# A small weight loaded as 16 lines of 1 KB in place of 128 lines of 128 B, and ScalarE's pause moved one group ahead, in a LoRA projection on one core

## Chip, cores, metric

The kernel runs on one core of a Trainium2 chip. The time is the device time of one execution in microseconds (us). All runs in this document count as undisturbed ("fast"): each is within 1.5% of the fastest of its kernel. Differences of 0.1 to 0.3 us are the subject, so eleven kernels were timed in five rounds and seven in three, always beside the kernel before on the same chip. Kernels of different rounds ran on different chips; each is compared with the kernel before of its own rounds. A profile shows one execution, and times in us from the start of its span.

A few words used below. A *packet* is one piece that one of the core's 16 DMA engines moves; the trace records start, duration, size and queue of each. A *load* goes from HBM to the core's SBUF memory, a *store* the other way. `x` is cut into four *chunks* of 8 MB, a chunk into 16 *groups* of 4 rows per partition.

## The reference

```python
x: (16, 2048, 256)   W: (256, 256)   lora_A: (256, 16)   lora_B: (16, 256)   lora_E: (16,)   # float32
y = x_flat @ W + scale * ((x_flat @ lora_A) * lora_E) @ lora_B                                # scale = 1
```

33.6 MB of `x` come in and 33.6 MB of `y` go out.

## The kernel before

The kernel folds the low-rank part into one weight, `weff = W + (A * E) @ B`, and then multiplies every group of `x` by it. For this it needs A transposed: `a_sb` holds A, TensorE turns it, VectorE scales it. SyncE issues all large transfers in the order of a list, and each chunk has a home in SBUF that the result overwrites. There are three homes for four chunks.

```python
ORDER = [
    ("A",),
    ("L", 0, 0, 16), ("L", 0, 16, 40), ("L", 0, 40, 64),      # loads: chunk, first row, last row
    ("L", 1, 0, 32), ("L", 1, 32, 64),
    ("L", 2, 0, 64),
    ("S", 0, 0, 40), ("S", 0, 40, 64),                        # stores
    ("L", 3, 0, 32), ("L", 3, 32, 64),                        # wait for the stores of chunk 0
    ("S", 1, 0, 64), ("S", 2, 2, 62), ("S", 3, 0, 64),
]
...
a_sb = sbuf("a_sb", [P, KT, R], FP32)                         # 128 partitions x 2 rows x 16
...
def drain(engine, n):                                         # waits for chunk 2's load, then n drains
    for op, landed in loaded.items():
        if op[1:3] == HELD:                                   # HELD = (2, 0)
            engine.wait_ge(landed, 16)
    for _ in range(n):
        engine.drain()
...
for g in range(N_GROUPS):                                     # ScalarE
    c, b = g // GPC, g % GPC * CG
    if (c, b) == HELD:
        drain(scalar, SCALAR_DRAINS)                          # 22
    scalar.wait_ge(s_y, g + 1)
    scalar.copy(out=home(c)[:, b:b + CG, :], in_=psum_y[g % NY][:])...
...
for t in range(KT):                                           # TensorE turns A: 2 x 128 columns
    ins = tensor.transpose(psum_y[0][:R, t, :P], a_sb[:, t, :], ident[:])
```

GpSimd holds chunk 2 back until the first store has landed. GpSimd and VectorE run some drains, empty instructions (8 to 34 ns in the median), while they stand there, and ScalarE runs its own when it comes to chunk 2. They are there for what the trace shows behind them: three packets of 8 KB in the queue that the page calls "instruction" (q14), at 67.83, 67.84 and 84.82 us, each 3 to 5 us after an engine's drains. I call them fetches. ScalarE's drains halt once, for 0.35 us between the 21st and the 22nd, and I take this pause for the sign of its fetch; the drains are meant to bring both into a time in which the engine idles.

Of the kernel before, what the change touches and what calls it, by code (L numbers as in the profile page):

```python
# [7 lines left out]
P = 128  # L8
FP32 = mybir.dt.float32
# [4 lines left out]
ROWS = 64  # L14
# [24 lines left out]
HELD = (2, 0)  # L39
# [3 lines left out]

VECTOR_DRAINS = 12
GPSIMD_DRAINS = 10
SCALAR_DRAINS = 22

CG = 4
GPC = ROWS // CG
# [8 lines left out]
def kernel(  # L58
# [13 lines left out]
    N, K = x_flat.shape  # L72
    M = out_flat.shape[1]
    R = lora_B.shape[0]
    KT = K // P
# [5 lines left out]
    sbuf, psum, sem = nc.alloc_sbuf_tensor, nc.alloc_psum_tensor, tc.alloc_semaphore  # L81
# [3 lines left out]
    ident = sbuf("ident", [P, P], FP32)  # L85

    w_sb = sbuf("w_sb", [P, KT, M], FP32)
    a_sb = sbuf("a_sb", [P, KT, R], FP32)
    b_sb = sbuf("b_sb", [R, M], FP32)
    e_sb = sbuf("e_sb", [R, 1], FP32)  # L90
    ate = sbuf("ate", [R, KT, P], FP32)
# [2 lines left out]
    psum_y = [psum(f"psum_y{i}", [P, CG, M], FP32) for i in range(NY)]  # L94
# [24 lines left out]
    def home(c):  # L119
        return homes[c % N_HOMES]  # L120

    sync, gpsimd, scalar, vector, tensor = nc.sync, nc.gpsimd, nc.scalar, nc.vector, nc.tensor
# [20 lines left out]
    def sync_program():  # L143
        for n, op in enumerate(ORDER):
            if op[0] == "A":
                a = lora_A.rearrange("(q t) r -> q t r", t=KT)
                ins = sync.dma_start(out=a_sb[:], in_=a).then_inc(set_up_loaded["a"], 16)  # L147
                opening.append(ins.ins.name)
                continue
            kind, c, s, e = op  # L150
            at_home = home(c)[:, s:e, :]
            if kind == "L":
                for st in stored:
                    if st[1] == c - N_HOMES and st[2] < e and s < st[3]:
                        sync.wait_ge(stored[st], 16)
                ins = sync.dma_start(out=at_home, in_=x_chunks[c, :, s:e, :]).then_inc(loaded[op], 16)
                if n == 1:
                    opening.append(ins.ins.name)
            else:
                sync.wait_ge(s_done, ends.index((c * ROWS + e - 1) // CG) + 1)  # L160
                sync.dma_start(out=y_chunks[c, :, s:e, :], in_=at_home).then_inc(stored.get(op, stored_rest), 16)
        sync.wait_ge(shared_stored, 16 * len(SHARES))
# [7 lines left out]
    def drain(engine, n):  # L170
        for op, landed in loaded.items():
            if op[1:3] == HELD:
# [3 lines that stand above are left out]
# [32 lines left out]
    def scalar_program():  # L208
        for name, to, of in (
            ("w", w_sb, W.rearrange("(q t) m -> q t m", t=KT)),  # L210
            ("b", b_sb, lora_B),
            ("e", e_sb, lora_E[:, None]),
        ):
            ins = scalar.dma_start(out=to[:], in_=of).then_inc(set_up_loaded[name], 16)
            opening.append(ins.ins.name)
        for g in range(N_GROUPS):
            c, b = g // GPC, g % GPC * CG
            if (c, b) == HELD:
                drain(scalar, SCALAR_DRAINS)
            scalar.wait_ge(s_y, g + 1)  # L220
            scalar.copy(out=home(c)[:, b:b + CG, :], in_=psum_y[g % NY][:]).then_inc(s_free[(g + NY) % UNROLL], 1)  # L221
            if (c, b + CG) == (SHARED, ROWS):
                scalar.drain().then_inc(s_shared, 1)
            if g in ends:
                scalar.drain().then_inc(s_done, 1)  # L225
# [23 lines left out]
    def tensor_program():  # L249
        def turn(i, result=None):  # L250
            words = stage[i % NS][:].bitcast(FP32)
            staged = s_stage[i % UNROLL]
            for b in range(CG):
                if b == 0:
                    tensor.wait_ge(staged, 1)
                if b == CG - 1 and result is not None:
                    tensor.wait_ge(s_free[result % UNROLL], 1)
                ins = tensor.transpose(psum_xt[i % NT][:, b, :], words[:, b, :], ident[:])  # L258
                if b == 0:
                    ins.then_inc(staged, -1)  # L260
            ins.then_inc(s_turned, 1)

        def multiply(i):
            turned, free = s_xt[i % UNROLL], s_free[i % UNROLL]
            for b in range(CG):
                for t in range(KT):
                    if b == t == 0:
                        tensor.wait_ge(turned, 1)
                    ins = tensor.matmul(  # L269
                        psum_y[i % NY][:, b, :],  # L270
                        xt[i % NX][:, b, t::KT],
                        weff[:, t, :],
                        start=(t == 0),
                        stop=(t == KT - 1),
                    )
                    if b == 0:
                        ins.then_inc((turned, free)[t], -1)
            ins.then_inc(s_y, 1)

        tensor.wait_ge(s_ident, 2)  # L280
        for i in range(WARM_UP):
            tensor.matmul(psum_y[1][:, :2, :], ident[:], ident[:, None, :].to_broadcast([P, 4, P]), start=True, stop=True)  # L282
        tensor.wait_ge(set_up_loaded["a"], 16)
        for t in range(KT):
            ins = tensor.transpose(psum_y[0][:R, t, :P], a_sb[:, t, :], ident[:])  # L285
        ins.then_inc(s_pe_set_up, 1)
        turn(0)
        tensor.wait_ge(set_up_loaded["b"], 16)
        tensor.wait_ge(s_ate, 1)
        for t in range(KT):  # L290
            ins = tensor.matmul(psum_y[1][:, t, :], ate[:, t, :], b_sb[:], start=True, stop=True)  # L291
        ins.then_inc(s_pe_set_up, 1)
        assert N_GROUPS % UNROLL == 0 and all(UNROLL % n == 0 for n in (NS, NX, NT, NY))
        with tensor.Fori(0, N_GROUPS // UNROLL):
            for i in range(UNROLL):
                turn(i + 1, i)
                multiply(i)
# [6 lines left out]
    with tc.tile_critical(no_gpsimd_drain=True):  # L304
        sync_program()
        gpsimd_program()
        scalar_program()
        vector_program()
        tensor_program()
# [35 lines left out]
```

## Time and profile before

| | before |
|---|---|
| median time (3 runs ahead of the prediction) | 161.29 us |
| bytes moved | 67.43 MB |
| floor (an estimate) at 27.1 GB/s per DMA engine, from 65,536 B in 2.418 us | 155.5 us |
| TensorE busy | 60% |
| share of SyncE's queue in the time of the 16 DMA engines | 97.4% |

The DMA engines move data from 1.0 us on without a visible gap (no slice of the page's DMA row is under 6), and TensorE stands idle for over a third of the time while they do (56 to 76 us, and from 122 us on). The page's chain of waits nevertheless names TensorE first:

```profile
PE 38%; DMA 33%; ACT 3%; POOL 1%; issue 1%; ACTq 0%; SPq 0%
```

A chain follows instructions and their semaphores. It can't see that a store, once issued, stands behind other stores in the queue.

### The profile page before, as it was taken

To read this page: it belongs to the slowest core of one execution; us is meant where nothing else is said; L and a number is where in the kernel's file an instruction comes from. 1 tells how busy PE (TensorE), PEld (TensorE's weight loads), DVE (VectorE), ACT (ScalarE), POOL (GpSimd) and SP (SyncE) were. 2 spreads that over 40 slices of the span, in tenths; PEclk is the share of its full clock that TensorE was granted. 3 is DMA by queue.
4 is the path that set the end of the run, shared out by engine and by line. 5 is a ranking of instruction groups with operands and counts; after the bars stand their busy time and mean duration, and the time that the engine had idled before them with its cause. 6 is when DMAs were issued, how large, how long until landed. Compare 5 with 4: busy or idle time off the path is not lost.

```text
span 160.0 us, 2070 instructions
## 1 busy us (share of the span) xinstructions
PE 96.5 (60%) x782; PEld 84.4 (53%) x782; DVE 45.4 (28%) x66; ACT 66.0 (41%) x65; POOL 69.3 (43%) x73
## 2 busy tenths in 40 slices
PE   2769999999999900000999999999994000000000
PEld 1246899999999900000789999999993000000000
DVE  0113355555555500000155555555550000000000
ACT  3001477777777720000257777777775000000000
POOL 1072577777787400002577777778762000000000
PEclk9999999999999995555599999999999555555555
DMA  7999999999969997999999999989979997989986
GB/s 269 427 448 436 412 440 467 451 393 418 631 262 524 475 311 328 403 420 434 412 465 428 401 475 426 532 377 410 524 308 446 480 485 305 544 342 481 441 360 262
DMA packets 2451, 67.43 MB, mean 421 GB/s; under 512 B 512, under 2 KB 528, under 8 KB 784
## 3 DMA queue, kind: packets, MB, share of 16 engines
q1 hardware_dynamic: 2016, 66.60, 97.4%
q0 software_dynamic: 224, 0.52, 0.9%
q10 hardware_dynamic: 208, 0.28, 0.6%
q14 instruction: 3, 0.02, 0.0%
HBM read 33.85 MB, written 33.55 MB: 421 GB/s over the span
## 4 chain that ended last, share of the span: by engine, by line
PE 38%; DMA 33%; ACT 3%; POOL 1%; issue 1%; ACTq 0%; SPq 0%
DMA out_dram<-home 28%; PE psum_y L269 24%; PE psum_xt L258 13%; DMA home<-in_x_dram 5%; ACT home L221 3%; POOL stage L200 1%; PE psum_y L291 1%; SPq L147 0%; ACTq L175 0%; ACTq L225 0%
## 5 line engine op out<-in xcount | busy, mean ns | idle before, releaser
L200 POOL CAST stage<-home 128x1024 bf16<-128x1024 f32 x64 | 66.6, 1042 | 48.6 <-PE psum_xt L258 22.1
L221 ACT COPY home<-psum_y 128x1024 f32<-128x1024 f32 x64 | 64.7, 1012 | 54.8 <-PE psum_y L269 54.8
L269 PE MATMUL psum_y<-weff,xt 128*128 128x256 bf16 x512 | 69.1, 280 | 0.0
L242 DVE COPY xt<-psum_xt 128x1024 bf16<-128x1024 bf16 x64 | 44.3, 692 | 66.2 <-PE psum_xt L258 66.2
L258 PE MATMUL psum_xt<-ident,stage 128*128 128x128 f32 x260 | 42.2, 286 | 22.3 <-POOL stage L200 22.3
L269 PEld LDWEIGHTS psum_y<-weff,xt 128*128 128x128 bf16 x512 | 51.5, 101 | 6.2
L258 PEld LDWEIGHTS psum_xt<-ident,stage 128*128 128x128 f32 x260 | 32.4, 148 | 25.2 <-issue 23.6
L282 PE MATMUL psum_y<-ident 128*128 128x512 f32 x4 | 3.8, 1101 | 2.9 <-POOL ident L180 2.9
L282 PEld LDWEIGHTS psum_y<-ident 128*128 128x128 f32 x4 | 1.2, 325 | 3.9 <-POOL ident L180 2.9
L230 DVE TENSOR_SCALAR ate<-psum_y,e_sb 16x256 f32<-16x256 f32 x1 | 0.5, 471 | 7.2 <-DMA e_sb<-in_lora_E_dram 7.2
L168 POOL DMA_DIRECT2D out_dram<-home x3 | 2.0, 676 | 1.0 <-PE psum_xt L258 1.0
L221 ACT ACT_TABLE_LOAD x1 | 1.3, 1283 | 2.1 <-SPq L304 2.1
L291 PE MATMUL psum_y<-b_sb,ate 16*128 16x256 f32 x4 | 2.1, 670 | 0.0
L291 PEld LDWEIGHTS psum_y<-b_sb,ate 16*128 16x128 f32 x4 | 1.2, 320 | 0.5 <-issue 0.3
L246 DVE TENSOR_TENSOR weff<-w_sb,psum_y 128x512 bf16<-128x512 f32 x1 | 0.7, 689 | 1.4 <-PE psum_y L291 1.4
L285 PEld LDWEIGHTS psum_y<-ident,a_sb 128*16 128x16 f32 x2 | 0.3, 138 | 1.2 <-issue 1.2
L178 POOL MEMSET ident<- 128x128 f32 x1 | 0.2, 205 | 1.7 <-SPq L304 1.7
L285 PE MATMUL psum_y<-ident,a_sb 128*16 128x128 f32 x2 | 0.6, 421 | 0.0
L180 POOL TENSOR_SCALAR_AFFINE_SELECT ident<-ident 128x128 f32<-128x128 f32 x1 | 0.3, 284 | 0.2 <-POOL ident L178 0.2
L326 POOL MEMSET const-float32-0.0<- 128x1 f32 x1 | 0.1, 94 | 0.2 <-issue 0.2
L326 POOL MEMSET const-bfloat16-1.0<- 128x1 bf16 x1 | 0.1, 97 | 0.0
L326 POOL MEMSET const-uint8-127<- 128x1 uint8 x1 | 0.1, 97 | 0.0
(1 smaller groups left out, 0.1 us busy)
## 6 DMA issues: line engine op xcount, KB each, us to landing
home<-in_x_dram SPq DMA_DIRECT2D x4, 4096.0 KB, 24.4
out_dram<-home SPq DMA_DIRECT2D x1, 7680.0 KB, 38.0
home<-in_x_dram SPq DMA_DIRECT2D x2, 3072.0 KB, 16.8
out_dram<-home SPq DMA_DIRECT2D x1, 5120.0 KB, 45.2
out_dram<-home SPq DMA_DIRECT2D x1, 3072.0 KB, 44.6
home<-in_x_dram SPq DMA_DIRECT2D x1, 2048.0 KB, 7.7
out_dram<-home POOLq DMA_DIRECT2D x1, 432.0 KB, 30.2
w_sb<-in_W_dram ACTq DMA_DIRECT2D x1, 256.0 KB, 2.8
```

The source lines that it names most:

```text
L168: engine.dma_start(out=ends_of(y_chunks[SHARED]), in_=ends_of(home(SHARED))).then_inc(landed, 16)
L200: gpsimd.tensor_copy(out=stage[g % NS][:], in_=home(c)[:, b:b + CG, :]).then_inc(s_stage[g % UNROLL], 1)
L221: scalar.copy(out=home(c)[:, b:b + CG, :], in_=psum_y[g % NY][:]).then_inc(s_free[(g + NY) % UNROLL], 1)
L230: vector.tensor_scalar(out=ate[:], in0=psum_y[0][:R, :KT, :P], scalar1=e_sb[:], scalar2=float(scale), op0=ALU.mult, op1=ALU.mult,).then_in ...
L242: vector.tensor_copy(out=xt[g % NX][:], in_=psum_xt[g % NT][:].bitcast(BF16)).then_inc(s_xt[g % UNROLL], 1)
L246: vector.tensor_add(out=weff[:], in0=w_sb[:], in1=psum_y[1][:, :KT, :]).then_inc(s_free[0], 1)
L258: ins = tensor.transpose(psum_xt[i % NT][:, b, :], words[:, b, :], ident[:])
L269: ins = tensor.matmul(psum_y[i % NY][:, b, :], xt[i % NX][:, b, t::KT], weff[:, t, :], start=(t == 0), stop=(t == KT - 1),)
L282: tensor.matmul(psum_y[1][:, :2, :], ident[:], ident[:, None, :].to_broadcast([P, 4, P]), start=True, stop=True)
L285: ins = tensor.transpose(psum_y[0][:R, t, :P], a_sb[:, t, :], ident[:])
L291: ins = tensor.matmul(psum_y[1][:, t, :], ate[:, t, :], b_sb[:], start=True, stop=True)
L326: nc = _bacc.Bacc("TRN2", target_bir_lowering=False, num_devices=1)
```

## The change

The intent is to free the start of the DMA stream. A's 16 KB come as 128 pieces of 128 B, eight on each DMA engine, ahead of the first `x` load. Now they come as 16 pieces of 1 KB, one per engine. Each partition then holds 16 rows of A, so TensorE turns A in 16 parts of 16 columns with a strided output. The second part of the change moves ScalarE's drains ahead of the copy of group 31, where ScalarE idles anyway, and takes 26 in place of 22, so that the pause still falls among them.

```diff
-SCALAR_DRAINS = 22
+SCALAR_DRAINS = 26
+
+A_ROWS = 16
 ...
-    a_sb = sbuf("a_sb", [P, KT, R], FP32)
+    a_sb = sbuf("a_sb", [K // A_ROWS, A_ROWS, R], FP32)
 ...
-                a = lora_A.rearrange("(q t) r -> q t r", t=KT)
+                a = lora_A.rearrange("(q j) r -> q j r", j=A_ROWS)
 ...
-            if (c, b) == HELD:
+            if (c, b + CG) in (HELD, (HELD[0] - 1, HELD[1] + ROWS)):
                 drain(scalar, SCALAR_DRAINS)
 ...
-        for t in range(KT):
-            ins = tensor.transpose(psum_y[0][:R, t, :P], a_sb[:, t, :], ident[:])
+        n_a = K // A_ROWS
+        for j in range(A_ROWS):
+            at = psum_y[0][:R, j % KT, j // KT:P:A_ROWS // KT]
+            ins = tensor.transpose(at, a_sb[:, j, :], ident[:n_a, :n_a])
```

## The prediction

Where a cut is marked in this text, or in an expectation further on, a statement on the hardware stood that no run here shows. 0.09 + 0.24 = 0.33 us, and 161.29 - 0.33 = 160.96. The 8 KB packets are the fetches named above.

> **What bounds the kernel now.** I read four views. First the page's slices, to see which resource is never free:
>
> ```profile
> span 160.0 us, 2070 instructions
> ...
> PE   2769999999999900000999999999994000000000
> ...
> DMA  7999999999969997999999999989979997989986
> ...
> DMA packets 2451, 67.43 MB, mean 421 GB/s; under 512 B 512, under 2 KB 528, under 8 KB 784
> ...
> q1 hardware_dynamic: 2016, 66.60, 97.4%
> ```
>
> The reader is to see that TensorE is idle for five slices in the middle and nine at the end, while the 16 DMA engines have a 9 almost everywhere. (A packet is booked in the slice in which it starts, so a 6 or 7 beside slices of 60 KB packets is booking, not idleness.) SyncE's queue q1 holds nearly all of it. The floor is worked out: a 65,536 B packet takes 2.418 us in the trace's packet records, 27.1 GB/s for one engine; 67.43 MB over 16 engines at that speed is 155.5 us. The first packet starts at 1.00 us and the last data packet ends at 159.66 us, so 158.7 us are spent on work whose floor is 155.5.
>
> Second, the DMA issues, to see whether a store's time is work or queueing:
>
> ```profile
> out_dram<-home SPq DMA_DIRECT2D x1, 7680.0 KB, 38.0
> out_dram<-home SPq DMA_DIRECT2D x1, 5120.0 KB, 45.2
> ...
> home<-in_x_dram SPq DMA_DIRECT2D x1, 2048.0 KB, 7.7
> ...
> a_sb<-in_lora_A_dram SPq DMA_DIRECT2D x1, 16.0 KB, 2.4
> ```
>
> The 7,680 KB store (chunk 2) needs 7.86 MB / 421 GB/s = 18.7 us and takes 38.0; the other 19 us it stands in the queue. The packet records say the same: the stores of chunks 1, 2 and 3 are issued at 82.8, 101.9 and 122.8 us, and their first packets start at 100.4, 119.7 and 138.8 us. So every store is ready 16 to 18 us before the DMA engines get to it. The page's chain of waits makes the opposite look true: it gives TensorE 38% of the span because it follows the last store back to ScalarE's last copy at 121.75. That copy could have come 16 us later without moving the end. The kernel is one unbroken DMA stream, and its end is the stream's start plus its length.
>
> Third, that start, in the windows view (columns: window, its length, busy time by engine, granted clock, DMA share, GB/s):
>
> ```profile
> 0.00:1.00 1.00, 0.00 (x0) 0.00 (x0) 0.00 (x0) 0.00 (x0) 0.20 (x4) 1.00 0.00 0
> 1.00:1.20 0.20, 0.00 (x0) 0.00 (x0) 0.00 (x0) 0.00 (x0) 0.00 (x0) 1.00 0.56 116
> 1.20:1.40 0.20, 0.00 (x0) 0.00 (x0) 0.00 (x0) 0.00 (x0) 0.00 (x0) 1.00 0.93 205
> 1.40:1.60 0.20, 0.00 (x0) 0.00 (x0) 0.00 (x0) 0.00 (x0) 0.00 (x0) 1.00 0.91 164
> 1.60:1.80 0.20, 0.00 (x0) 0.00 (x0) 0.00 (x0) 0.00 (x0) 0.00 (x0) 1.00 0.25 67
> 1.80:2.00 0.20, 0.00 (x0) 0.00 (x0) 0.00 (x0) 0.00 (x0) 0.00 (x0) 1.00 1.64 554
> ```
>
> In the first 0.8 us of the stream 0.2 x (116+205+164+67) = 110 KB move, 138 GB/s; at 430 they would need 0.26 us. About 0.54 us is lost here, in the stretch in which A's 128 B lines and W's 2 KB lines are moved. The engines count as busy (0.91): several W packets take 340 to 480 ns where their usual time is 84, and all of those end near 1.82 to 1.99 us.
>
> Fourth, the timeline of ScalarE and TensorE where chunk 2 is let go:
>
> ```profile
> 79.11 1.01 ACT L221 COPY home<-psum_y 128x1024 f32<-128x1024 f32 x1 [21.80 <-PE psum_y L269]
> 79.72 1.11 PE L269 MATMUL psum_y<-weff,xt 128*128 128x256 bf16 x8
> 81.45 1.93 ACT L221 COPY home<-psum_y 128x1024 f32<-128x1024 f32 x2 [1.33 <-PE psum_y L269]
> 82.52 0.14 PEld L258 LDWEIGHTS psum_xt<-ident,stage 128*128 128x128 f32 x1 [0.29 <-ACT home L221]
> ```
>
> ScalarE idles 1.33 us between the copies of groups 31 and 32. The view names TensorE, but that matmul ended near 80.8: it is the 22 drains (80.23 to 81.42) that hold the copy. TensorE loses 0.29 us to it.
>
> [...] The trace has A's 128 packets of 128 B at 11 to 13 ns, where 128 B at 27.1 GB/s is 4.7 ns. [...] the first x packet on any engine starts at 1.88 us[...] and every later load and store starts in the order of issue. [...] The trace has three such 8 KB packets, two at 67.83 us, 4.5 us after VectorE's and GpSimd's drains, and one at 84.82, after ScalarE's.
>
> **Part by part.** *A's load.* Before: 128 packets, 8 on each engine, 8 x 11.9 = 0.10 us of packet time, in practice 0.14 us (one engine: first at 1.001, the next work at 1.153). After: one 1 KB packet per engine; the 16 KB of B have this form and took 46 ns each. Saved directly: 0.14 - 0.05 = 0.09 us. Behind it stands the stall. If A's small writes cause it, the stretch up to 1.8 us loses most of its 0.54; if W's first reads from memory cause it, nothing of it goes. I count a bit under half of it: 0.24. Sum: 0.33 us, and since nothing else on the DMA stream gives way, it goes to the end one for one.
>
> *The 16 turns.* Two transposes of 128 columns (0.21 us apart, finished by 7.09 us) become 16 of 16 columns. A pair of weight load and matmul in the loop takes 0.87 / 8 = 0.11 us, a weight load of 16 columns 138 ns: 16 x 0.11 to 0.14 = 1.8 to 2.2 us, less at best. They still begin behind the warm-up at 6.45 and end at 8.3 to 8.7; VectorE's scaling (0.47 us) ends by 9.2. Its user, the product with B, stands behind the first group's turn, which ends at 10.42. So at most nothing is added, and any addition would lie in the 16 us of slack.
>
> *The drains.* 22 become 26 and move ahead of group 31's copy. They wait for chunk 2's load (landed at 62.7 us) and then run while ScalarE is idle anyway (57.3 to 79.1). Group 31 has two instructions, so copy 32 stands 4 later; the pause that marks the fetch, between drains 21 and 22, falls on drain 24 of 26, still inside. The fetch moves from 84.8 to about 67.8: same 8 KB, same 0.31 us on one engine. Copy 32 can start when its matmuls end, 80.85, so ScalarE gains 0.6 us and TensorE 0.3. Both lie in the slack: 0.00 at the end.
>
> Total: 161.29 - 0.33 = 160.96, say 160.95.
>
> **Rivals.** *Nothing moves* (161.2 to 161.3): the stall belongs to W or to the start of the stream, and the time freed by A is idle, since W's first packet comes at 1.153 us whatever A does. For it: W's issue, not A's end, sets 1.153, and A's own packet time is only 0.10. Against it: some of A's packets are still served at 1.66 to 1.98[...]. *The whole stall goes* (160.6 to 160.7): for it, 0.54 us of low rate end just as A's last packets do. *Compute becomes the bound* (slower): it would need over 16 us. [...] I give it 1%. *The tail shifts*: the engines end between 158.7 and 159.7 us, and earlier GpSimd stores or the moved fetch could change which ends last, by some 0.1 us either way.
>
> **Range and chances.** The two ends of A's saving are 0.05 and 0.60; with the tail's 0.1 that is 160.6 to 161.25, and I take 160.65 to 161.25 for 8 in 10. A change of 2% would be 3.2 us, six times all that is lost at the start. Faster 0.005, within 2% 0.985, slower 0.01.
>
> **What would show it.** Packets fall by 112 to 2339, and those under 512 B from 512 to 384. A lands in about 2.1 us and the first x load in about 7.4 instead of 7.7; the windows from 1.0 to 1.8 us carry over 138 GB/s. The turns are one row of 16 matmuls ending before 8.7 us, and the product with B still follows the first group's turn. ScalarE's drains stand at 62.7 us, its gap of 1.33 before copy 32 falls to some 0.7, and the third fetch comes near 67.8. The last packets all come about 0.33 us sooner, with the DMA row unchanged. I am wrong if the first x load lands as late as before, if the start is sooner but the end isn't, or if TensorE's set-up delays the first group's product.

## The result

The changed kernel takes 161.25 us (161.10 to 161.57, 6 runs) against 161.28 us of the kernel before (6 runs). Ratios in this document are the mean time of one kernel's fast runs over that of the other's of the same rounds, so they are not quite the ratio of the medians quoted. Here the ratio is 1.0003, with a 95% interval from 0.9989 to 1.0017. The 0.33 us that I expected did not come.

The page of the changed kernel, its slices and packet counts:

```profile
span 160.0 us, 2102 instructions
...
PE   2769999999999700000899999999996000000000
...
DMA  7999999999969997999999999998998998999976
...
DMA packets 2339, 67.43 MB, mean 421 GB/s; under 512 B 384, under 2 KB 416, under 8 KB 672
```

The 128 small packets of A are gone: 2451 - 112 = 2339, and 384 are left under 512 B. The span is what it was.

Its DMA issues (size, median time from issue to landing):

```profile
out_dram<-home SPq DMA_DIRECT2D x1, 7680.0 KB, 37.1
...
out_dram<-home SPq DMA_DIRECT2D x1, 5120.0 KB, 46.5
...
home<-in_x_dram SPq DMA_DIRECT2D x1, 2048.0 KB, 7.6
...
a_sb<-in_lora_A_dram SPq DMA_DIRECT2D x1, 16.0 KB, 2.3
```

A lands after 2.3 us in place of 2.4, the first `x` load after 7.6 in place of 7.7. The mean over the 16 engines of that load's last packet, from the packet records, is 7.39 us in both kernels. The 5 MB store is an instructive line. In this run its issue came at 28.74 us, 1.12 us sooner than before, since TensorE's clock happened to rise earlier (17.29 us, before 18.42; in both, a group's 8 matmuls take 1.71 us ahead of it and 0.87 after). It took 1.3 us longer from issue to landing, so it landed at 75.2 us, before at 75.1: when this store was issued did not matter.

The windows of the start, same columns as in the prediction:

```profile
1.00:1.20 0.20, 0.00 (x0) 0.00 (x0) 0.00 (x0) 0.00 (x0) 0.00 (x0) 1.00 1.25 113
1.20:1.40 0.20, 0.00 (x0) 0.00 (x0) 0.00 (x0) 0.00 (x0) 0.00 (x0) 1.00 0.82 61
1.40:1.60 0.20, 0.00 (x0) 0.00 (x0) 0.00 (x0) 0.00 (x0) 0.00 (x0) 1.00 0.05 20
1.60:1.80 0.20, 0.00 (x0) 0.00 (x0) 0.00 (x0) 0.00 (x0) 0.00 (x0) 1.00 0.32 118
1.80:2.00 0.20, 0.00 (x0) 0.00 (x0) 0.00 (x0) 0.00 (x0) 0.00 (x0) 1.00 1.02 384
```

The stretch up to 1.8 us is still nearly empty; the bytes of the packets that start in it are even fewer, 0.2 x (113 + 61 + 20 + 118) = 62 KB against 110 KB. W's first packet starts at 1.161 us (before 1.153), and its slow packets now take up to 598 ns and end between 1.57 and 1.94 us (before: 1.75 to 1.99). The gap has not gone with A's small packets. It has only got other packets in it.

The group of TensorE's turns of A, and ScalarE's drains, by source line:

```profile
L289 PEld LDWEIGHTS psum_y<-ident,a_sb x16: 84/86/89, 6.6 to 7.0; 16*16 16x16 f32 x16
L289 PE MATMUL psum_y<-ident,a_sb x16: 180/183/191, 6.6 to 7.0; 16*16 16x16 f32 x16
```

```profile
L177 ACTq DRAIN  x26: 8/8/143, 62.5 to 63.8; - x26
```

The 16 turns take 0.59 us from 6.59 us on, no longer than the two did (0.64). The drains stand at 62.5 us as intended. The timeline where chunk 2 is let go, of the changed kernel:

```profile
79.33 1.01 ACT L223 COPY home<-psum_y 128x1024 f32<-128x1024 f32 x1 [23.13 <-PE psum_y L271]
79.94 1.91 PE L271 MATMUL psum_y<-weff,xt 128*128 128x256 bf16 x8
81.89 1.01 ACT L223 COPY home<-psum_y 128x1024 f32<-128x1024 f32 x1 [1.55 <-PE psum_y L271]
```

ScalarE still idles 1.55 us between the copies of groups 31 and 32. This time it is TensorE: its matmuls take 1.91 us in place of 1.11, because in this run the clock, granted at 0.50 until then, was granted in full again only at 82.14 us (before: 79.86).

### The profile page after: what moved, and what is told of

Same layout as the page of the kernel before. It is cut to its first block, busy times and chain, and to the rows that moved or that the text cites. A ratio compares the mean times of both kernels' runs of the same rounds, so it can differ in the third digit from the quotient of the medians.

```text
span 160.0 us, 2102 instructions
## 1 busy us (share of the span) xinstructions
PE 96.3 (60%) x796; PEld 84.5 (53%) x796; DVE 45.4 (28%) x66; ACT 66.1 (41%) x65; POOL 69.2 (43%) x73
## 2 busy tenths in 40 slices
DMA packets 2339, 67.43 MB, mean 421 GB/s; under 512 B 384, under 2 KB 416, under 8 KB 672
## 4 chain that ended last, share of the span: by engine, by line
PE 40%; DMA 34%; POOL 1%; ACT 1%; issue 0%; SPq 0%; ACTq 0%
DMA out_dram<-home 29%; PE psum_y L271 26%; PE psum_xt L260 14%; DMA home<-in_x_dram 5%; POOL stage L202 1%; ACT home L223 1%; PE psum_y L295 1%; SPq L149 0%; ACTq L227 0%
## 5 line engine op out<-in xcount | busy, mean ns | idle before, releaser
L271 PE MATMUL psum_y<-weff,xt 128*128 128x256 bf16 x512 | 69.9, 282 | 0.0
L260 PE MATMUL psum_xt<-ident,stage 128*128 128x128 f32 x260 | 41.7, 285 | 23.5 <-POOL stage L202 23.4
L295 PE MATMUL psum_y<-b_sb,ate 16*128 16x256 f32 x4 | 1.5, 500 | 0.0
L289 PEld LDWEIGHTS psum_y<-ident,a_sb 16*16 16x16 f32 x16 | 0.5, 86 | 1.5 <-issue 1.5
L295 PEld LDWEIGHTS psum_y<-b_sb,ate 16*128 16x128 f32 x4 | 0.7, 194 | 0.2 <-issue 0.2
L289 PE MATMUL psum_y<-ident,a_sb 16*16 16x16 f32 x16 | 0.6, 183 | 0.0
```

What stands on the lines that cost most here:

```text
L260: ins = tensor.transpose(psum_xt[i % NT][:, b, :], words[:, b, :], ident[:])
L271: ins = tensor.matmul(psum_y[i % NY][:, b, :], xt[i % NX][:, b, t::KT], weff[:, t, :], start=(t == 0), stop=(t == KT - 1),)
L289: ins = tensor.transpose(at, a_sb[:, j, :], ident[:n_a, :n_a])
L295: ins = tensor.matmul(psum_y[1][:, t, :], ate[:, t, :], b_sb[:], start=True, stop=True)
```

## The experiments

Eighteen kernels were run. Except where it is said, results are correct. "Before" is always the kernel before in the same rounds. "End of chunk 2's load" and the like are means over the 16 engines, from the packet records.

### The two parts alone

`a_only` is the changed kernel with `SCALAR_DRAINS = 22` and `if (c, b) == HELD:`. `drains_only` is the kernel before with the 26 drains in the new place.

> Only A's load and its turns are changed; the 22 drains stand where they stood before. Theory (A's small packets are served in a gap in which the DMA engines wait for W's first data anyway, so A's form costs nothing): 161.25 us, within 0.15 of before, and the first x load ends at 7.4 us on the average of the 16 engines as in both profiles. Rival (A's form does save 0.1 to 0.3 us, and the moved drains with their earlier instruction fetch give it back): 0.1 to 0.3 us faster than before.

> Only ScalarE's drains are changed; A is loaded as before. Theory (ScalarE has 16 us of slack against the DMA stream, and the fetch is the same 8 KB): within 0.15 us of before. Rival (the moved fetch costs what A's form saves): 0.1 to 0.3 us slower than before.

| | median | before | ratio (95%) |
|---|---|---|---|
| a_only | 161.36 | 161.14 | 1.0015 (1.0002 to 1.0029) |
| drains_only | 161.02 | 161.14 | 0.9996 (0.9982 to 1.0009) |

Neither part gains, so nothing was gained by one and lost by the other; A's new form alone is if anything slower, by some 0.2 us at an interval that only just leaves out zero. In `drains_only` the clock came back at 80.17 us, near where it did before (79.86), and ScalarE's gap shrank from 1.33 to 0.86 us as the prediction's reasoning wanted. The time did not follow.

### What the start of the stream waits for

`w_late` moves W's load from ScalarE's queue behind the first `x` load on SyncE's.

```diff
     ("L", 0, 0, 16),
+    ("W",),                       # issued by SyncE; taken out of ScalarE's list
 ...
```

> The changed kernel with W's load moved from ScalarE's queue to SyncE's, behind the first x load, so that x's 16 KB lines come right after A. Theory 1 (the gap of some 0.6 us up to 1.8 us is the delay of the first large reads, whoever asks for them): the x packets now show the gap, and the time stays within 0.15 us of before. Theory 2 (the gap belongs to W's 2 KB lines, or to two queues at once): x's first packets start near 1.5 us and the time falls by 0.3 to 0.5 us.

It takes 161.51 us against 161.14, ratio 1.0020 (1.0007 to 1.0034): slower. The windows of `w_late` at the start:

```profile
1.40:1.80 0.40, 0.00 (x0) 0.00 (x0) 0.00 (x0) 0.23 (x1) 0.18 (x1) 1.00 2.56 620
1.80:2.20 0.40, 0.00 (x0) 0.00 (x0) 0.00 (x0) 0.40 (x1) 0.16 (x2) 1.00 0.15 41
2.20:2.60 0.40, 0.20 (x1) 0.20 (x2) 0.00 (x0) 0.40 (x1) 0.14 (x1) 1.00 0.24 82
```

The first `x` packet of each engine starts between 1.48 and 1.87 us; a 16 KB packet later takes 0.61 us, so the engines ought to start the next ones from 2.1 us on. But these first ones take 0.66 to 1.26 us, and only two more start before 2.6. The gap is now in `x`, with W nowhere near, and it begins later because the first large load arrives at 1.48 us in place of 1.16. So in these runs the gap is paid by the first large load, be it W or `x`, from the moment when its packets arrive. That was theory 1; its "within 0.15 us" was too narrow. The lateness that came with the later gap stayed: chunk 1's load ends at 41.68 us, 0.30 us later than in the changed kernel.

`no_w` takes W's load away and sets W to zero in the core, so its result is wrong.

```diff
-            ("w", w_sb, W.rearrange("(q t) m -> q t m", t=KT)),
 ...
+        vector.memset(w_sb[:], 0.0).then_inc(set_up_loaded["w"], 1)
 ...
```

> The changed kernel without W's load; W is set to zero in the core, so the result is wrong on purpose. 256 KB less, 0.6 us of the stream, gone at its start. If what is saved at the start reaches the end: 0.6 us faster than before. If the wait on the last packets of chunk 2's load near 61.5 us takes it up (as it took up the 0.5 us that 8 copies of A added): that wait grows by about 0.6 us and the time stays within 0.2 us of before.

It takes 160.92 us against 161.25, ratio 0.9980 (0.9966 to 0.9993). The first `x` load ends at 7.24 us, only 0.15 us sooner than with W, though 0.6 us of work are gone: the gap has moved into `x` as in `w_late`. Of 0.6 us, 0.33 reached the end. Neither of the two outcomes was met: most of the 0.6 us was gone by the end of the first `x` load already, and the wait before the first store did not grow by 0.6 us; it was 0.94 us, in the changed kernel 1.11 (how it is measured is said below).

### What a line of A costs

One load of A is too small to measure at the end, so these kernels read A 8 or 24 times over in its one load, into chunk 2's home, which is filled later. SyncE holds the load of chunk 2 until A has been turned.

```diff
 # narrow_8, on the kernel before (narrow_24 with 24)
-                a = lora_A.rearrange("(q t) r -> q t r", t=KT)
+                a = lora_A.rearrange("(q t) r -> q (t r)", t=KT)[:, None, :].to_broadcast([P, 8, KT * R])
 ...
 # wide_8, on the changed kernel (wide_24 with 24)
-                a = lora_A.rearrange("(q j) r -> q j r", j=A_ROWS)
+                a = lora_A.rearrange("(q j) r -> q (j r)", j=A_ROWS)[:, None, :].to_broadcast([16, 8, A_ROWS * R])
 ...
```

> The kernel before, with A read 8 times over by its one load (128 x 8 lines of 128 B; the copies land in the buffer of chunk 2, which is loaded later). 64 packets per engine at 12.3 ns are 0.79 us. Theory (A is served in a gap that ends near 1.8 us): 0 to 0.4 us slower than before. Rival (every small packet costs its time at the end): 0.7 to 1.0 us slower.

> The same with 24 copies: 192 packets per engine, 2.36 us. Past the gap the packets must show: from 8 to 24 copies the time grows by 16 x 0.098 = 1.6 us if the trace's 12.3 ns is the whole cost of a 128 B packet[...]. Theory: 1.6 to 2.0 us slower than before. Rival: 2.3 to 3.2 us slower.

> The changed kernel with A read 8 times over as 16 x 8 lines of 1 KB: 8 packets per engine at 44 ns, 0.35 us, all inside the gap. Theory: within 0.15 us of before. Rival: 0.2 to 0.3 us slower than the changed kernel.

> The same with 24 copies: 1.06 us of packets per engine. Theory (0.6 to 0.8 us of it in the gap): 0.2 to 0.5 us slower than before. Rival: 0.9 to 1.1 us slower. From 8 to 24 copies at most 16 x 0.044 = 0.7 us, under half of what the narrow form adds.

| | median (before 161.24) | ratio (95%) | end of the first x load | wait at the end of chunk 2's load |
|---|---|---|---|---|
| kernel before | | | 7.39 | 1.25 |
| narrow_8 | 161.43 | 1.0010 (0.9993 to 1.0027) | 7.97 | 0.61 |
| narrow_24 | 163.65 | 1.0152 (1.0135 to 1.0169) | 9.98 | 0.98 |
| changed kernel | | | 7.39 | 1.11 |
| wide_8 | 161.49 | 1.0021 (1.0005 to 1.0038) | 7.91 | 0.77 |
| wide_24 | 163.45 | 1.0141 (1.0123 to 1.0158) | 10.56 | 0.03 |

`narrow_8` is in the theory's range (0.19 us slower), `narrow_24` in the rival's (2.4 us). `wide_8` is 0.25 us slower than the kernel before, which is nearer to the rival's (that named the changed kernel, which was not in these rounds), and `wide_24`, 2.2 us slower, is outside of both. So something was missing from both theories. From 8 to 24 copies the first `x` load moves by (9.98 - 7.97) / 16 = 0.126 us per copy in the narrow form, and by (10.56 - 7.91) / 16 = 0.166 us in the wide one. I had expected 0.044. The wide form is not cheaper at all. (At the end the slopes are 0.139 and 0.123 us, but there the last column interferes.) The last column, in us, is the subject of the part after the next.

### Why 1 KB lines are no cheaper

A 1 KB packet of A takes 44 ns in the median of the changed kernel's 16, and 46 with 8 copies, but 76 with 24 copies (158 in `adjacent_23` below). My guess was that the partitions matter that the lines go to. To test this, two kernels load A once as changed and then 23 times more into a buffer that nobody reads, in the same form; one into partitions 0 to 15, the other into partitions 0, 8, 16 to 120. The 0.15 us per copy agree with `wide_24`, which has 23 copies more than the changed kernel: its first `x` load ends 10.56 - 7.39 = 3.17 us later, 0.14 us per copy, and its A lands 6.2 - 2.3 = 3.9 us later, 0.17. The "1 to 2 us sooner" was my estimate.

```diff
+                ins = sync.dma_start(out=homes[2][:16, :23, :], in_=more).then_inc(more_a, 16)    # adjacent_23
+                ins = sync.dma_start(out=homes[2][::8, :23, :], in_=more).then_inc(more_a, 16)    # spread_23
```

> The changed kernel with a second load of A behind the first: 23 copies as lines of 1 KB into partitions 0 to 15 of chunk 2's buffer (not read). Control for spread_23, with the same extra issue of 0.4 us on SyncE. Theory [...]: the copies take 23 x 0.15 = 3.5 us to land, as in the run with 24 copies, and the first x load lands 3 to 4 us later than in the changed kernel.

> The same, but the 16 lines go to partitions 0, 8, 16 to 120[...]. Nothing else differs. [...] the first x load lands 1 to 2 us sooner than in adjacent_23. Rival (1 KB packets or re-reading the same 16 KB of HBM are slow by themselves): no difference from adjacent_23 within 0.3 us.

The issue rows of the second load, first `adjacent_23`, then `spread_23`:

```profile
home<-in_lora_A_dram SPq DMA_DIRECT2D x1, 368.0 KB, 7.7
```

```profile
home<-in_lora_A_dram SPq DMA_DIRECT2D x1, 368.0 KB, 4.6
```

The same bytes in the same lines land in 4.6 us in place of 7.7. The median packet falls from 158 to 46 ns, the first `x` load ends at 10.68 in place of 11.79 us, and the time is 163.47 in place of 164.43 us. Only the partitions differ, so 1.1 us at the first `x` load and 1.0 us at the end are theirs. That is a part of the cost: in `wide_24`, with the same 24 copies in one load, the first `x` load ends at 10.56 us, so the second issue costs too, and with the lines spread it still ends later than in `narrow_24` (9.98). That spread lines beat small ones is not shown, nor what it is in the partitions that sets the packets' time. For the single copy of the changed kernel none of this can be seen: 13 of its 16 packets took 44 to 46 ns, as the 1 KB packets of B do (46).

### Why the start does not carry to the end

In `narrow_8` the first `x` load ended 0.58 us later than before, yet chunk 2's load ended at 61.93 us in both. The packet records show where: in nearly every run the last packets of chunk 2's load, one of 64 KB on each of the 16 engines, take mostly 3 to 3.9 us in place of 2.42. The windows view shows it as a stretch in which no packet starts. Of the kernel before, then of `wide_24`:

```profile
58.00:58.60 0.60, 0.00 (x0) 0.00 (x0) 0.00 (x0) 0.00 (x0) 0.00 (x0) 1.00 6.08 1748
58.60:61.50 2.90, 0.00 (x0) 0.00 (x0) 0.00 (x0) 0.00 (x0) 0.00 (x0) 0.64 0.00 0
```

```profile
61.40:61.70 0.30, 0.00 (x0) 0.00 (x0) 0.00 (x0) 0.00 (x0) 0.00 (x0) 0.65 8.07 3495
61.70:63.80 2.10, 0.00 (x0) 0.00 (x0) 0.00 (x0) 0.00 (x0) 0.00 (x0) 0.50 0.00 0
63.80:64.10 0.30, 0.00 (x0) 0.00 (x0) 0.00 (x0) 0.00 (x0) 0.00 (x0) 0.50 5.13 2192
```

Before, 16 packets start by 58.6 us and the next not until after 61.5, over 2.9 us later, though a packet needs 2.42. In `wide_24` the next follow at once. The wait of the table above is this excess: the time of the packets of chunk 2's load less their size over 27.1 GB/s, summed for each engine. In both kernels it is the largest single loss that I found in the stream, and it differs from kernel to kernel by more than the whole change was to bring. (The profile is one run of each; I don't know its spread between runs of one kernel. Nor does the end of chunk 2's load decide all: the profiled run of `narrow_8`, its slowest at 161.74 us, had the same 61.93 us there, and its last data packet still ended 0.37 us later than before's.)

My first idea, "ring theory" in the texts below, was only a count, that of SyncE's packets on each engine ahead of the first store. The waiting runs had 56 to 65, 119 or 247 of them, the three runs without wait (`wide_24`, `adjacent_23`, `spread_23`) had 79 or 80. Four kernels put that count at or near 80 without a late start. `narrow_3` is `narrow_8` with 3 copies. The others load chunk 1 in four parts:

```diff
-    ("L", 1, 0, 32), ("L", 1, 32, 64),
+    ("L", 1, 0, 16), ("L", 1, 16, 32), ("L", 1, 32, 48), ("L", 1, 48, 64),
```

> The kernel before with three copies of A as 128 B lines: SyncE's queue has 24 + 1 packets of A per engine and 54 of x before the first store, 79, the number at which the wait was absent. Packet time at the start grows by 16 x 12 ns = 0.2 us. Ring theory: the last packets of chunk 2's load take 2.42 us, and the end comes 0.8 to 1.2 us sooner than before, 160.1 to 160.5 us. Rival (the wait is chance, or fell away because the start was 3 us late): last packets 3 us or more, and 161.1 to 161.5 us.

> The changed kernel with chunk 1 loaded in four parts of 16 rows in place of two of 32: 2 + 72 = 74 packets per engine before the first store in place of 56, no bytes more. Ring theory: the wait at the end of chunk 2's load falls from 1.1 to under 0.2 us and the time to 160.1 to 160.5 us. Rival: the wait stays at 0.6 to 1.3 us and the time within 0.2 us of before.

> The kernel before with the same split: 9 + 72 = 81 packets. Ring theory: 160.1 to 160.5 us, as l1_split, which says that A's form is worth nothing without the wait either (within 0.15 us of l1_split). Rival: as before.

> x_first with the same split of chunk 1: 74 packets. x_first already lost half of the wait (0.59 us) and came to 160.83. Ring theory: the rest goes too, 160.1 to 160.4 us. Rival: 160.7 to 161.0, as x_first.

| | count | median (before 161.15) | ratio (95%) | wait |
|---|---|---|---|---|
| narrow_3 | 79 | 161.33 | 1.0014 (1.0000 to 1.0027) | 0.84 |
| l1_split | 74 | 161.08 | 0.9998 (0.9985 to 1.0012) | 0.82 |
| l1_split_b | 81 | 160.94 | 0.9987 (0.9974 to 1.0001) | 1.03 |
| x_first_split | 74 | 160.92 | 0.9985 (0.9971 to 0.9998) | 0.29 |

The wait stays in all four, 160.1 to 160.5 us came in none: the count is out. `s0_early` asks whether the wait belongs to that moment or to the change from loads to stores, and moves the first store ahead of the second half of chunk 2's load.

```diff
-    ("L", 2, 0, 64),
-    ("S", 0, 0, 40),
+    ("L", 2, 0, 32),
+    ("S", 0, 0, 40),
+    ("L", 2, 32, 64),
```

> The changed kernel with chunk 2 loaded in two halves and the first store (40 rows of chunk 0) put between them. If the wait belongs to the first change from loads to stores, the last packets of the first half (near 51 us) wait some 1 us and those of the second half don't. If it belongs to the end of chunk 2's load, or to the time when compute is idle, the first half's packets take their 1.21 us and the wait stays near 61 us or later. Time within 0.3 us of before in both; half the load waits less on its buffer, but the DMA stream moves the same bytes.

It takes 161.57 us against 161.19, ratio 1.0019 (1.0007 to 1.0031). Its windows:

```profile
49.90:50.50 0.60, 0.60 (x8) 0.54 (x6) 0.52 (x1) 0.60 (x1) 0.49 (x1) 1.00 3.21 874
50.50:51.80 1.30, 1.30 (x14) 1.21 (x13) 0.68 (x2) 1.00 (x2) 1.03 (x2) 1.00 0.00 0
51.80:52.40 0.60, 0.60 (x8) 0.58 (x6) 0.18 (x1) 0.30 (x2) 0.56 (x1) 1.00 2.54 1092
```

A wait now comes ahead of the moved store: the last 32 KB packets of the first half take 1.8 to 2.0 us in place of 1.21, and the excess of that half is 0.97 us, while compute is at full work. So in this run it is not tied to 61.5 us nor to idle engines, but to loads that a store follows. It is not tied to the first store alone: against what I had written down, a second one of 0.74 us came with the second half, so the extra change between loads and stores cost as well. Yet at the change from chunk 3's loads to the next store, near 101 us, the last packets took only 0.00 to 0.24 us too long in the mean, over all twenty profiles. What sets the size of the wait stays open.

### Compute's slack

`warm_8` is the changed kernel with `WARM_UP = 8`.

> The changed kernel with 8 warm-up matmuls on TensorE in place of 2, which holds the set-up back by 6 x 0.85 to 1.7 = 5 to 10 us. If compute has 16 us of slack against the DMA stream, the first copy of ScalarE comes 5 us or more later and the time stays within 0.15 us of the changed kernel. If compute is on the path, the time grows by those 5 us.

The 0.85 us are the distance of two warm-up matmuls in the trace before; 1.7 is an estimate, twice that, from the groups of 8 matmuls that take 1.71 us at one time and 0.87 at another.

161.33 us against 161.14, ratio 1.0013 (0.9998 to 1.0028). This test failed as a test: TensorE was at its faster rate sooner (the copies of ScalarE follow each other after 1.31 us from the first on, in the changed kernel after 2.56 and 1.56 us at first; that the warm-up is the reason isn't shown), the first copy of ScalarE came at 15.82 us, only 1.4 us later than in the changed kernel and not 5, and the first store was issued at 28.69 us, as early as there. The next kernels say more on the slack: `x_first` issues its first store 2 us later than the changed kernel and is faster than the kernel before.

### A version that beats both

`x_first` is the changed kernel with the first `x` load ahead of A; `x_first_b` is the same order on the kernel before.

```diff
-    ("A",),
     ("L", 0, 0, 16),
+    ("A",),
```

> The changed kernel with the first x load issued ahead of A on SyncE. A then lands behind 2 MB of x, near 7.4 us, and the set-up follows later, which the 16 us of slack cover. Theory (the delay of the first large reads is paid once, from the moment they arrive): x's packets arrive 0.15 us sooner than W's did, the first x load lands 0.1 to 0.2 us sooner, and the end moves by that at most, so within 0.2 us of before. Rival (A ahead of x costs the stream something): 0.3 us or more faster.

> The kernel before with the first x load issued ahead of A, A in its old form. If the gain of x_first comes from the order alone: 160.7 to 161.0 us, 0.2 to 0.5 us faster than before, as x_first. If A's wide form has a part in it (its 128 small packets now stand between two x loads, at 12 ns each 0.1 us): 0.1 us or more slower than x_first.

| | median | before | ratio (95%) | wait |
|---|---|---|---|---|
| x_first | 160.83 | 161.25 | 0.9976 (0.9963 to 0.9990) | 0.59 |
| x_first_b | 160.84 | 161.19 | 0.9981 (0.9968 to 0.9994) | 0.47 |

Both are faster than the kernel before by some 0.2% (the changed kernel has the same time as that one, and was not in these rounds), and A's form makes no difference that shows. The windows of `x_first`:

```profile
1.00:1.40 0.40, 0.00 (x0) 0.00 (x0) 0.00 (x0) 0.00 (x0) 0.00 (x0) 1.00 2.72 614
1.40:1.80 0.40, 0.00 (x0) 0.00 (x0) 0.00 (x0) 0.00 (x0) 0.00 (x0) 1.00 0.15 41
```

`x` now arrives at 1.0 us and pays the gap from there. That is what I wanted of it, but it is not shown to be the cause of the gain: W and A come behind the first load, and chunk 1's load ends at 41.52 us, 0.14 us later than in the changed kernel. The gain appears only at the wait before the first store, which is 0.59, 0.47 and 0.29 us in the three kernels that have `x` first, and 0.82 to 1.29 in the profiled kernels with A first whose start was not made later by many copies of A. I can't say why.

## Why the prediction was wrong, point by point

- **What bounds the kernel** was right. The DMA stream decides: what delayed its start by 2 us or more came out at the end for the most part (`narrow_24`, `wide_24`, `adjacent_23`, `spread_23`), and neither the stores' issue nor ScalarE's pause reaches the end: `drains_only` changed ScalarE's gap and not the time, and the first store of the changed kernel was issued 1.12 us sooner and landed no sooner.
- **"Saved directly: 0.14 - 0.05 = 0.09 us"** failed, but not by the packet time, which was nearly as I took it (13 of 16 packets at 44 to 46 ns). The time that A freed was not used: W's first packet starts at 1.161 us, before at 1.153, and 62 KB in place of 110 start moving up to 1.8 us. As a rate it was wrong too: with many copies, the wide form costs 0.166 us per copy and the narrow one 0.126, and `spread_23` shows that a part of this comes from the partitions.
- **"I count a bit under half of it: 0.24"** is the step that failed, and the larger part of the 0.33 us. I had given A's small packets a share in the stall up to 1.8 us. It stayed when they were gone: the first `x` load ends at 7.39 us in both kernels. `w_late` and `no_w` show that the first large load pays it. Of my rivals, "nothing moves" was the one that came true, with this reason ("or to the start of the stream").
- **"It goes to the end one for one"** had nothing to carry here, and is no safe rule. In `w_late` it held about (0.30 us later at the end of chunk 1's load, 0.37 us at the end), in `no_w` too (0.25 us sooner there in the profile, 0.33 us at the end). In `narrow_8` it did not: it began 0.58 us later and reached the end of chunk 2's load at the same moment, since the wait before the first store was 0.61 us and not 1.25. I had seen those long packets as part of 3 us of general loss and had not asked where they were.
- **The 16 turns** were oversized: 0.59 us in place of 1.8 to 2.2. I took the time of one weight load as the distance of two; a pair of 16 columns follows the last after 27 ns (the 16 start between 6.59 and 7.00 us, 0.41 / 15). It lay in the slack, as said.
- **The drains**: time and place, the fetch (packets at 67.70 to 67.93 us in place of one at 84.82) and the worth of nothing were right. The gap of ScalarE was to fall to 0.7 us; it fell to 0.86 in `drains_only` and rose to 1.55 in the changed kernel, where the clock came back 2.3 us later.
- **The signs** that I named: packet counts right; A's landing 2.3 us and not 2.1; the first `x` load 7.6 us and not 7.4; the early windows carry less and not more. "I am wrong if the first x load lands as late as before" is what happened.
- **A reading** of the prediction was not quite right: of the long W packets (338 to 479 ns) one ends at 1.75 us, not all near 1.82 to 1.99. Nothing rests on it.

## What to carry to other kernels

Fewer and larger lines need not help a DMA, and where many of them go into a few neighbouring partitions they can cost more than small ones (0.166 against 0.126 us per copy here, and 7.7 us to land in neighbouring partitions against 4.6 in spread ones): when a small tensor is packed into few partitions, ask which ones. A low rate at the start of a stream is not the fault of what happens to be moved there until another order has been tried: let the largest load arrive first, and see whether the gap goes or only changes its tenant. And before a saving at one end of a DMA stream is carried to the other, list the places between where packets take longer than their size; a wait of 1 us there can swallow it (0.58 us in `narrow_8`, by the end of chunk 2's load).

## What the runs show beyond the change

- Whether 16 large or 128 small packets are faster for the same bytes: for 16 KB here, no difference at the end (161.25 and 161.28 us), and with many copies 0.166 us per copy for 16 lines of 1 KB in partitions 0 to 15 against 0.126 for 128 lines of 128 B. It depends on the partitions: 4.6 us in place of 7.7 to land with the lines spread.
- 0.126 us per copy over 8 packets per engine is 16 ns per 128 B packet: over three times the 4.7 ns of 128 B at 27.1 GB/s, but close to the 11 to 13 ns that the packet records show, so hardly any cost stands behind them that those records don't show.
- The wait of the last loads before the first store: 0.03 to 1.29 us in these runs, and near 52 us in place of 61.5 where the first store was moved ahead.
- The first large load of the stream stalls once in these runs: after some 0.2 to 0.4 us of packets the 16 engines start few packets or none for about half a microsecond, and the packets under way take longer (16 KB up to 1.26 us in place of 0.61 in `w_late`), whether it is W (1.2 to 1.8 us) or `x` (1.9 to 2.5 us in `w_late`, 1.4 to 2.1 in `x_first`).
- Each of the eleven profiles whose queues I listed has three fetches of 8,192 B, each a single packet. Of these only `warm_8` has one of 16,384 B as well, at 158.83 us; which engine it served, the trace does not say.
